# The load of the weight group two places on, tied behind the adding transfer of the next group

## The chip, the cores and the metric

The kernel runs on one core of a Trainium2 chip. The metric is the device time of one execution in microseconds: before the change the median of three runs is 1652.49 us (1649.63 to 1653.38). Engines are named as in the profile: PE (TensorE matmul), DVE (VectorE), ACT (ScalarE), POOL (GpSimd) and SP (SyncE). POOL, SP and ACT also issue DMA transfers.

## The reference

Two layers of a hybrid decoder over 512 tokens of width 2048, in float32. Each layer normalises its input, projects it with one wide matrix, runs three mixers side by side (a short gated convolution, a stick-breaking attention of 8 heads of 128, and a gated linear attention, GLA, of 4 heads), and projects their concatenation back into the residual stream.

```python
h = _rmsnorm(x, norm_g)
proj = h @ w_in
# proj is split into: cv_h cv_b cv_c cv_g | sb_q sb_k sb_v sb_g | gl_q gl_k gl_v gl_g gl_lr
y_conv = _short_conv(cv_h, cv_b, cv_c, conv_w, conv_b) * silu(cv_g)
q, k = _rmsnorm(sb_q, sb_qn_g), _rmsnorm(sb_k, sb_kn_g)
y_sb = _stick_breaking(q, k, sb_v) * silu(sb_g)
g = log_sigmoid(gl_lr @ gla_w_up + gla_b_up) / 16
y_gla = _rmsnorm(_gla(gl_q, gl_k, gl_v, g), gla_on_g) * silu(gl_g)
return x + concatenate([y_conv, y_sb, y_gla]) @ w_out
```

## The kernel before

The weights stream from HBM in groups of 256 columns (2048 x 256 float32, 2 MB, tile `st`, two buffers). `specs` lists them in the order of use: in each layer six groups of the GLA, then conv h 0, c 0, g 0, b 0, then for j = 0 to 3 the attention's v j, g j, q j and k j (two heads each), then conv h 1, c 1, g 1, b 1, and eight groups of `w_out`. I call the group by these names.

Each float32 operand is split into two float16 parts, and a product is three float16 matmuls. Two ways exist. A plain group (`project_cols`, `project_toks`; the values' groups v j and conv h 1 are such) multiplies directly. A group in `quick` (every g j, q j and k j of the attention, and some of the convolution) uses seven half-size products of sums of quarter blocks instead of eight (`project_quick`, lines 763 to 807: L778 and L781 are its matmuls).

What a weight group goes through, by lines:

- `fetch(i)` loads it in two halves of 1 MB (L360), issued on POOL's queue for all but the first three groups.
- `wmax(i, h)` squares it on ACT in two passes and sums (L379); for a quick group, between the two passes, POOL issues the **adding transfer** (L382): a DMA inside `st` that adds the left 128 columns of every second row block to the right 128 columns, in place. It is one of the sums that the seven products need, done by DMA.
- `wscale(i)` reduces the sums across partitions on POOL (L395, `wgm`) and makes a power-of-two scale on DVE (L398, L407, L411 `ws`, L413 `wu`).
- A plain group is then split by `whi` and `wlo` (L450 on ACT, L457 on DVE). A quick group is split by `wsums`: each of seven blocks goes through L500 on ACT (high part) and L501 on DVE (low part), with sums of blocks between them (L520, L522, L525 on DVE). L520 reads what the adding transfer wrote. The first two blocks don't need it.

When a group's matmuls begin, `weights()` takes it and does two things for the groups behind it: it issues the load of the group two places on (into the buffer that the group in use has left free, since its parts are split by then), and puts into `hooks` the squares and the scale and split of the next group, which are emitted behind the group's first matmul and behind a matmul in its middle.

In the attention, PE runs v j, then scores of heads of the pair before (L1249), g j, scores, q j, values (L1289), k j, values. Keys and queries of 512 tokens are normalised on DVE (L217 to L222, L1344 to L1357), split (L1361 on ACT, L1362 on DVE) and transposed by DMAs that SP issues (L1366: `qT<-qp` the queries, `kT<-raw` the keys). So in the values' group v j+1 the keys of pair j are being normalised and transposed, the weights of g j+1 are being scaled and split, and the scores of pair j follow right behind the group. `mixd` transfers (L900) are finished mixer outputs on their way to HBM, on POOL's queue too.

The order on each engine comes from a scheduler that orders instructions by a simulated timeline. What is emitted inside `tc.high_priority()` is preferred. `order(a, b)` makes the scheduler place a behind b; between two engines it adds no wait at run time, on one engine it fixes their order.

Of the kernel before, what the change touches and what calls it, by code (L numbers as in the profile page):

```python
# [11 lines left out]
ALU = mybir.AluOpType  # L12
# [5 lines left out]
P = 128  # L18
# [25 lines left out]
def hybrid_trunk(ctx, tc, x, norm_g, w_in, conv_w, conv_b, sb_qn_g, sb_kn_g,  # L44
                 gla_w_up, gla_b_up, gla_on_g, w_out, out):
    nc = tc.nc
    V, S, G, T = nc.vector, nc.scalar, nc.gpsimd, nc.tensor
# [4 lines left out]
    HK = KT // 2  # L52
    GW = 256
# [17 lines left out]
    def nm(s):  # L71
        uid[0] += 1
        return f"{s}_{uid[0]}"

    def sm(n, tag, bufs=None):
        return small.tile([P, n], F32, tag=tag, name=nm(tag), bufs=bufs or 1 + (tag in TWICE))

    def wk(shape, tag, bufs=None, dt=F32):
        return work.tile(shape, dt, tag=tag, name=nm(tag), bufs=bufs)
# [115 lines left out]
    def order(a, b):  # L195
        tc.add_manual_dep(a.ins, b.ins.name, mybir.DependencyInfo(
            mybir.DependencyClass.NoSync, mybir.DependencyReason.DATA), reason="order")
# [116 lines left out]

    quick = set()
    specs = []

    def spec(name, l, src, cols):
        if name in (QUICK[l] if src is w_out else QUICK_IN):
            quick.add(len(specs))  # L320
        specs.append((l, src, cols))

    for l in range(depth):
        for name, cols in (("gla v 0", [(GL_V, GW)]), ("gla v 1", [(GL_V + GW, GW), (GL_LR, LR)]),
# [19 lines left out]
    staged, whole, narrow, peak, scales = {}, {}, {}, {}, {}  # L344

    def junk(n):

        return wk([P, HK * GX], "junk", 1, dt=U8)[:, :n]


    def fetch(i):

        l, src, cols = specs[i]
        queue = nc.gpsimd if i > 2 else nc.sync
        staged[i] = st = []
        whole[i] = stage.tile([P, KT, GW], F32, tag="st", name=nm("st"))
        for h in range(2):
            s_ = whole[i][:, h * HK:(h + 1) * HK, :]
            c0 = cols[0][0]
            queue.dma_start(s_, src[l, h * HK * P:(h + 1) * HK * P, c0:c0 + GW].rearrange("(k p) n -> p k n", p=P),  # L360
                            max_dma_last_dim=1024)
            st.append(s_)
        if len(cols) > 1:
            c0, w = cols[1]
            narrow[i] = wk([P, KT, w], "kT")
            nc.sync.dma_start(narrow[i], src[l, :, c0:c0 + w].rearrange("(k p) n -> p k n", p=P))

    def early(i):
        return i in quick and specs[i][1] is not w_out

    def wmax(i, h):

        if h == 0:
            peak[i] = sm(2 + (i in narrow), "wm")
        if early(i):
            part = whole[i][:, :, (1 - h) * P:(2 - h) * P]
        else:
            part = staged[i][h]
        sq = S.activation(junk(HK * GW).rearrange("p (k n) -> p k n", k=part.shape[1]), part, AF.Square,  # L379
                          accum_out=peak[i][:, h:h + 1])  # L380
        if early(i) and not h:
            G.dma_start(out=whole[i][:, ::2, P:], in_=whole[i][:, ::2, :P], accum_op=ALU.add)  # L382
        if h and i in narrow:
            S.activation(junk(KT * LR).rearrange("p (k n) -> p k n", k=KT), narrow[i], AF.Square,
                         accum_out=peak[i][:, 2:3])
        return sq
# [55 lines left out]
        else:  # L442
            V.tensor_scalar(wh[:, ks, :GW], staged[0][h][:, ks, :GW], scales[0], None, ALU.mult)

    hooks, lastmm = [], [None]

    def whi(i, h):
        wh = wpool.tile([P, HK, GX], F16, tag="wh", name=nm("wh"))
        wl = wpool.tile([P, HK, GX], F16, tag="wl", name=nm("wl"))
        hi = S.activation(wh[:, :, :GW], staged[i][h], AF.Copy, scale=scales[i])  # L450
        if i in narrow:
            S.activation(wh[:, :, GW:], narrow[i][:, h * HK:(h + 1) * HK, :], AF.Copy, scale=scales[i])
        loaded[i][0].append((wh, wl))
# [8 lines left out]
    def squares(i, mm):  # L462

        with tc.high_priority():
            for h in range(2):
                a = wmax(i, h)
                if not h:
                    order(a, mm)

    def parts_of(i, mm):  # L470

        with tc.high_priority():
            order(wscale(i), mm)
            if i in quick:
                wsums(i)
                return
            for h in range(2):
                whi(i, h)
                wlo(i, h)
# [49 lines left out]
    def weights():  # L529

        i = cursor[0]
        cursor[0] += 1
        if i + 2 < len(specs):
            with tc.high_priority():
                fetch(i + 2)
        assert not hooks
        if i and i + 1 < len(specs):
            hooks.extend([lambda mm: squares(i + 1, mm), lambda mm: parts_of(i + 1, mm)])
        return loaded.pop(i)

    fetch(0)
# [128 lines left out]
    for l in range(depth):  # L670
# [207 lines left out]
        def mixscale(j, m, tag, top=11.0):  # L878

            pow2(pmix[:, j:j + 1], m, -top, tag)  # L880
            s_ = sm(1, tag + "smix")
            V.reciprocal(s_, pmix[:, j:j + 1])
            return s_
# [103 lines left out]
        for tag in ("qT", "kT"):  # L987
# [10 lines left out]
            s_ = sm(1, "gas")  # L998
# [41 lines left out]
        for p in range(2):  # L1040
# [53 lines left out]
            for two, bias in ((0, (nT[:, p, 0:1], None, nT[:, p, 2:3], None)),  # L1094
                              (1, (nT01[:, p:p + 1], nT[:, p, 1:2], None, nT[:, p, 2:3]))):
                e = wk([P, 2, 256], "e")
                n = [0, 0]
# [201 lines left out]
        for j in range(4):  # L1299
# [17 lines left out]
            s_ = mixscale(2 + j, m, "b", 12.0)  # L1317
# [140 lines left out]
```

## Time and profile before

| | |
|---|---|
| median of three runs | 1652.49 us (1649.63 to 1653.38) |
| the profiled execution's own time | 1652.11 us |
| its span, first to last instruction | 1650.3 us |
| granted PE clock, mean | 0.999 |
| bytes moved by DMA | 234.90 MB, mean 142 GB/s |
| of them by POOL's queue (q0) | 177.22 MB, 39.9% of 16 engines' span |
| loads of `w_in` on POOL's queue (L360) | 114 halves of 1 MB |
| adding transfers (L382) | 34 of 512 KB |

A profile's span is given as busy time of each engine and as the idle time ahead of each instruction with what ended it. A row of a timeline reads: start and length in us, engine, line, operation, what it writes and reads, shape, how often, and in brackets the idle time of the engine ahead of it and what ended it. A row that ends in "x2" merges two equal ones. A row of POOL or SP with DMA in its name is the time of the issue, not of the transfer. A row of the waits reads: who waited, for what, in total, how often, the longest.

### The profile page before, as it was taken

To read this page: it belongs to the slowest core of one execution; us is meant where nothing else is said; L and a number is where in the kernel's file an instruction comes from. 1 tells how busy PE (TensorE), PEld (TensorE's weight loads), DVE (VectorE), ACT (ScalarE), POOL (GpSimd) and SP (SyncE) were. 2 spreads that over 40 slices of the span, in tenths; PEclk is the share of its full clock that TensorE was granted. 3 is DMA by queue.
4 is the path that set the end of the run, shared out by engine and by line. 5 is a ranking of instruction groups with operands and counts; after the bars stand their busy time and mean duration, and the time that the engine had idled before them with its cause. 6 is when DMAs were issued, how large, how long until landed. Compare 5 with 4: busy or idle time off the path is not lost.

```text
span 1650.3 us, 41607 instructions
## 1 busy us (share of the span) xinstructions
PE 1621.0 (98%) x17914; PEld 1341.0 (81%) x17914; DVE 1415.1 (86%) x2377; ACT 1185.3 (72%) x1743; POOL 270.0 (16%) x298
## 2 busy tenths in 40 slices
PE   7999999999999999999999999999999999999999
PEld 5746668988999968789986467689898989668998
DVE  7977989969797979798689689898898989888893
ACT  8667787857777776756765687788786868666571
POOL 0121121111212121111112112112121212111110
PEclk9999999999999999999999999999999999999999
DMA  7144344496767686644543442635777766683441
GB/s 260 58 150 122 70 133 86 111 159 148 167 148 167 148 167 175 170 157 149 193 141 104 115 116 66 178 78 151 148 163 150 161 155 150 158 229 129 154 155 53
DMA packets 193913, 234.90 MB, mean 142 GB/s; under 512 B 90226, under 2 KB 154044, under 8 KB 193216
## 3 DMA queue, kind: packets, MB, share of 16 engines
q0 software_dynamic: 76992, 177.22, 39.9%
q1 hardware_dynamic: 107728, 45.56, 13.7%
q10 hardware_dynamic: 9008, 9.45, 1.8%
q8 instruction: 140, 2.29, 0.6%
q14 instruction: 45, 0.37, 0.1%
HBM read 179.65 MB, written 14.68 MB: 118 GB/s over the span
## 4 chain that ended last, share of the span: by engine, by line
PE 40%; DVE 5%; ACT 3%; DMA 1%; issue 1%; POOL 0%; DVEq 0%; ACTq 0%; POOLq 0%
PE psp L781 11%; PE psp L778 7%; PE psp L828 5%; PE psp L697 3%; PE psp L698 3%; PE psp L699 3%; PE psp L686 3%; PE psp L687 3%; PE psp L688 2%; DVE wl L501 1%; ACT junk L379 1%; ACT wh L500 1%; DVE za L1265 1%; PE psm L1289 1%; DMA st<-in_w_in_dram 1%
## 5 line engine op out<-in xcount | busy, mean ns | idle before, releaser
L500 ACT ACTIVATE wh<-st,ws 128x1024 f16<-128x1024 f32 x252 | 281.7, 1147 | 194.0 <-DVE st L520 96.7
L501 DVE SCALAR_TENSOR_TENSOR wl<-st,ws,wh 128x1024 f16<-128x1024 f32 x252 | 318.0, 1283 | 37.9 <-ACT wh L500 37.8
L379 ACT ACTIVATE junk<-st 128x2048 uint8<-128x2048 f32 x150 | 285.7, 1905 | 16.7 <-DMA st<-in_w_in_dram 8.5
L778 PE MATMUL psp<-s,wh 128*128 128x256 f16 x1152 | 195.6, 273 | 0.0
L778 PEld LDWEIGHTS <-wh 128*128 128x128 f16 x1728 | 168.3, 98 | 22.4 <-issue 2.1
L781 PE MATMUL psp<-wh,s 128*128 128x128 f16 x2048 | 176.7, 219 | 0.0
L697 PE MATMUL psp<-wh,m 128*128 128x256 f16 x640 | 174.5, 273 | 0.0
L698 PE MATMUL psp<-wl,m 128*128 128x256 f16 x640 | 174.5, 273 | 0.0
L699 PE MATMUL psp<-wh,m 128*128 128x256 f16 x640 | 174.5, 273 | 0.0
L781 PE MATMUL psp<-wl,s 128*128 128x128 f16 x1024 | 173.2, 219 | 0.0
L781 PEld LDWEIGHTS <-s 128*128 128x128 f16 x3072 | 172.9, 98 | 0.0
L457 DVE SCALAR_TENSOR_TENSOR wl<-st,ws,wh 128x2048 f16<-128x2048 f32 x68 | 158.9, 2347 | 14.7 <-ACT wh L450 14.7
L450 ACT ACTIVATE wh<-st,ws 128x2048 f16<-128x2048 f32 x66 | 130.7, 1998 | 41.8 <-DVE ws L411 22.8
L360 POOL DMA_DIRECT2D st<-in_w_in_dram x114 | 102.7, 905 | 344.3 <-DVE w7l L501 119.9
L778 PE MATMUL psp<-s,wl 128*128 128x256 f16 x576 | 156.7, 273 | 0.0
L395 POOL PARTITION_ALL_REDUCE wgm<-wm x75 | 54.3, 724 | 489.9 <-ACT junk L379 477.2
L781 PEld LDWEIGHTS <-m 128*128 128x128 f16 x2304 | 131.1, 98 | 2.2 <-issue 1.6
L382 POOL DMA_DIRECT2D st<-st x34 | 53.8, 1584 | 276.5 <-ACT junk L379 236.1
L778 PEld LDWEIGHTS <-wl 128*128 128x128 f16 x864 | 84.5, 98 | 16.0 <-issue 6.0
L781 PE MATMUL psp<-wh,m 128*128 128x128 f16 x1024 | 91.5, 219 | 0.3 <-DVE raw L794 0.3
L781 PE MATMUL psp<-wl,m 128*128 128x128 f16 x512 | 87.5, 219 | 0.0
L688 PEld LDWEIGHTS <-wl 128*128 128x128 f16 x448 | 43.8, 98 | 53.7 <-DVE wl L457 2.3
(442 smaller groups left out, 4203.0 us busy)
## 6 DMA issues: line engine op xcount, KB each, us to landing
st<-in_w_in_dram POOLq DMA_DIRECT2D x114, 1024.0 KB, 8.2
st<-in_w_out_dram POOLq DMA_DIRECT2D x32, 1024.0 KB, 8.4
st<-st POOLq DMA_DIRECT2D x34, 512.0 KB, 7.0
st<-in_w_in_dram SPq DMA_DIRECT2D x6, 1024.0 KB, 11.8
mixd<-g POOLq DMA_DIRECT2D x20, 256.0 KB, 6.9
x<-in_x_dram SPq DMA_DIRECT2D x4, 1024.0 KB, 5.1
qT<-in_x_dram ACTq DMA_DIRECT2D x8, 512.0 KB, 6.2
qT<-xs ACTq DMA_DIRECT2D x8, 512.0 KB, 3.9
```

Of the source, the lines that this page charges most:

```text
L360: queue.dma_start(s_, src[l, h * HK * P:(h + 1) * HK * P, c0:c0 + GW].rearrange("(k p) n -> p k n", p=P), max_dma_last_dim=1024)
L379: sq = S.activation(junk(HK * GW).rearrange("p (k n) -> p k n", k=part.shape[1]), part, AF.Square, accum_out=peak[i][:, h:h + 1])
L450: hi = S.activation(wh[:, :, :GW], staged[i][h], AF.Copy, scale=scales[i])
L457: V.scalar_tensor_tensor(wl[:, :, :GW], staged[i][h], scales[i], wh[:, :, :GW], ALU.mult, ALU.subtract)
L500: hi = S.activation(h_, b, AF.Copy, scale=sc)
L501: V.scalar_tensor_tensor(l_, b, sc, h_, ALU.mult, ALU.subtract)
L697: T.matmul(o, ah[:, t, k, :], wh[:, kk, :n], start=st_, stop=False, skip_group_check=True)
L698: T.matmul(o, ah[:, t, k, :], wl[:, kk, :n], start=False, stop=False, skip_group_check=True)
L699: return T.matmul(o, al[:, t, k, :], wh[:, kk, :n], start=False, stop=en, skip_group_check=True)
L778: mm = T.matmul(o, w[q_][:, kk, :], a[p_][:, :, kk, :], start=st_, stop=en, skip_group_check=True)
L781: mm = T.matmul(o[:, t * P:(t + 1) * P], a[p_][:, t, kk, :], w[q_][:, kk, :], start=st_, stop=en, skip_group_check=True)
L828: mm = T.matmul(o[:, :n], a_[:, t, k, :], w[k // HK][part][:, k % HK, :n], start=i == 0 and k == 0, stop=i == 2 and k == KT - 1)
```

## The change

In the groups whose name begins with "v " and in conv h 1 (`held`), the load of the group two places on is no longer emitted at the start of `weights()`. It is emitted behind the group's first matmul, right after the next group's squares, with `order` behind the last adding transfer that was emitted (`added[0]`), which is that of the next group: g j, or conv c 1. All other groups load as before.

```diff
     quick = set()
     specs = []
+    names = []
 
     def spec(name, l, src, cols):
         if name in (QUICK[l] if src is w_out else QUICK_IN):
             quick.add(len(specs))
         specs.append((l, src, cols))
+        names.append(str(name))
...
-    def fetch(i):
+    def fetch(i, behind=None):
...
-            queue.dma_start(s_, src[l, h * HK * P:(h + 1) * HK * P, c0:c0 + GW].rearrange("(k p) n -> p k n", p=P),
-                            max_dma_last_dim=1024)
+            load = queue.dma_start(s_, src[l, h * HK * P:(h + 1) * HK * P, c0:c0 + GW].rearrange(
+                "(k p) n -> p k n", p=P), max_dma_last_dim=1024)
+            if behind is not None:
+                order(load, behind)
             st.append(s_)
...
         if early(i) and not h:
-            G.dma_start(out=whole[i][:, ::2, P:], in_=whole[i][:, ::2, :P], accum_op=ALU.add)
+            added[0] = G.dma_start(out=whole[i][:, ::2, P:], in_=whole[i][:, ::2, :P], accum_op=ALU.add)
...
-    hooks, lastmm = [], [None]
+    hooks, lastmm, added = [], [None], [None]
...
         i = cursor[0]
         cursor[0] += 1
-        if i + 2 < len(specs):
+        held = names[i][:2] == "v " or names[i] == "conv h 1"
+        if i + 2 < len(specs) and not held:
             with tc.high_priority():
                 fetch(i + 2)
         assert not hooks
+
+        def first(mm):
+            squares(i + 1, mm)
+            if held:
+                with tc.high_priority():
+                    fetch(i + 2, added[0])
+
         if i and i + 1 < len(specs):
-            hooks.extend([lambda mm: squares(i + 1, mm), lambda mm: parts_of(i + 1, mm)])
+            hooks.extend([first, lambda mm: parts_of(i + 1, mm)])
         return loaded.pop(i)
```

The built programs show what moves. The order of PE and of SP is the same in both. Line numbers of the changed kernel are 2 to 12 higher (L362 is L360 of before, L386 is L382, L399 is L395, L504 and L505 are L500 and L501, L1365 to L1374 are L1353 to L1362).

POOL in the values' group v 1 of layer 0, before: `st_4191` is the weight of g 1, `st_4599` that of q 1.

```order
L360 DMA st_4191<-in_w_in_dram 128x8x256 x2
L900 DMA mixd_187<-g_1488 1024x1x128
L360 DMA st_4599<-in_w_in_dram 128x8x256 x2
L382 DMA st_4191<-st_4191 128x8x128
L395 ISA wgm_4659<-wm_4607 128x2
L382 DMA st_4599<-st_4599 128x8x128
```

The same place in the changed kernel, where `st_4610` is the weight of q 1:

```order
L362 DMA st_4191<-in_w_in_dram 128x8x256 x2
L912 DMA mixd_187<-g_1488 1024x1x128
L386 DMA st_4191<-st_4191 128x8x128
L362 DMA st_4610<-in_w_in_dram 128x8x256 x2
L399 ISA wgm_4659<-wm_4604 128x2
L386 DMA st_4610<-st_4610 128x8x128
```

The load of q 1 and the adding transfer of g 1 have changed places; the reduction of g 1's maxima still follows both. The same swap stands in each of the ten held groups.

DVE in the same group, before: the end of the keys' norm (`qr`, `qrt`), the first low part of g 1 (`wl_4668`), then the scaling of the keys (L1357) and their low part (L1362).

```order
L222 SCALAR_TENSOR_TENSOR qr_467_4575<-qrt_4577,qr_467_4575 128x16
L220 TENSOR_TENSOR qrt_4577<-qr_467_4575 128x16
L501 SCALAR_TENSOR_TENSOR wl_4668<-st_4191,ws_4663,wh_4667 128x1024
L221 SCALAR_TENSOR_TENSOR qrt_4577<-qrt_4577,qrm_3777 128x16
L222 SCALAR_TENSOR_TENSOR qr_467_4575<-qrt_4577,qr_467_4575 128x16
L1353 TENSOR_SCALAR qz_4587<-qr_467_4575,qu_4181 128x8
L1355 TENSOR_SCALAR qr_467_4575<-qr_467_4575,wu_3893 128x8
L1354 TENSOR_SCALAR qz_4587<-qz_4587 128x8
L1357 TENSOR_TENSOR kT_4190<-kT_4190,qr_467_4575 128x1024
L1362 SCALAR_TENSOR_TENSOR raw_4592<-kT_4190,raw_4592 128x1024
```

The same place in the changed kernel:

```order
L222 SCALAR_TENSOR_TENSOR qr_467_4575<-qrt_4577,qr_467_4575 128x16
L220 TENSOR_TENSOR qrt_4577<-qr_467_4575 128x16
L221 SCALAR_TENSOR_TENSOR qrt_4577<-qrt_4577,qrm_3777 128x16
L222 SCALAR_TENSOR_TENSOR qr_467_4575<-qrt_4577,qr_467_4575 128x16
L1365 TENSOR_SCALAR qz_4587<-qr_467_4575,qu_4181 128x8
L505 SCALAR_TENSOR_TENSOR wl_4668<-st_4191,ws_4663,wh_4667 128x1024
L1367 TENSOR_SCALAR qr_467_4575<-qr_467_4575,wu_3893 128x8
L1366 TENSOR_SCALAR qz_4587<-qz_4587 128x8
L1369 TENSOR_TENSOR kT_4190<-kT_4190,qr_467_4575 128x1024
L1374 SCALAR_TENSOR_TENSOR raw_4592<-kT_4190,raw_4592 128x1024
```

The low part of g 1 stands three rows later, still ahead of the scaling of the keys. The four rows of g 1's scale (L398 to L413) stand a few rows later as well, between the steps of the norm.

ACT in the values' group v 2 of layer 0, before, with `wh` the high parts of g 2 and `raw` the high part of the keys of pair 1:

```order
L897 ACTIVATE g_3538<-e_6015,bsmix_3774 128x512
L500 ACTIVATE wh_6107<-st_5607,ws_6103 128x1024
L1361 ACTIVATE raw_6008<-kT_5606 128x1024
L500 ACTIVATE wh_6109<-st_5607,ws_6103 128x1024
L500 ACTIVATE wh_6107<-st_5607,ws_6103 128x1024
```

The same place in the changed kernel:

```order
L909 ACTIVATE g_3538<-e_6015,bsmix_3774 128x512
L1373 ACTIVATE raw_6008<-kT_5606 128x1024
L504 ACTIVATE wh_6107<-st_5607,ws_6103 128x1024
L504 ACTIVATE wh_6109<-st_5607,ws_6103 128x1024
L504 ACTIVATE wh_6107<-st_5607,ws_6103 128x1024
```

The split of the keys has gone ahead of the first high part. DVE follows it at this place: there L1357 and L1362 stand ahead of the first L501. So it is in v 2, v 3 and conv h 1 of both layers; v 0 has no difference on ACT or DVE.

## The prediction

> **What bounds the kernel now.** I read the page's busy times first, then the windows view over the stretches that the change touches, then the waits of PE, and last the timelines.
>
> ```profile
> PE 1621.0 (98%) x17914; PEld 1341.0 (81%) x17914; DVE 1415.1 (86%) x2377; ACT 1185.3 (72%) x1743; POOL 270.0 (16%) x298
> ```
>
> PE is busy for 1621.0 of 1650.3 us. Whatever the change does to loads, DVE or ACT counts only where PE waits, and the change doesn't touch the order of PE's instructions. So the question is where PE is idle in the changed stretches. The windows view answers it. Each row below is one stretch from the start of a values' group to the start of the next, or of conv h 1 (first column its bounds, then its length, then busy time of each engine): the first three begin with v 1, v 2 and v 3 of layer 0, the last three with those of layer 1.
>
> ```profile
> core 0: us, PE busy (x) PEld busy (x) DVE busy (x) ACT busy (x) POOL busy (x), PEclk, DMA share, GB/s
> 336.10:426.20 90.10, 84.29 (x1095) 78.00 (x1093) 74.04 (x123) 63.45 (x112) 15.21 (x18) 1.00 0.78 148
> 426.20:509.80 83.60, 83.60 (x1096) 77.95 (x1093) 74.36 (x124) 63.71 (x109) 16.32 (x18) 1.00 0.71 152
> 509.80:593.40 83.60, 83.60 (x1095) 77.95 (x1093) 74.33 (x124) 64.03 (x109) 16.52 (x18) 1.00 0.71 157
> 1150.50:1234.50 84.00, 83.66 (x1096) 77.96 (x1094) 74.20 (x123) 63.52 (x112) 15.42 (x18) 1.00 0.76 158
> 1234.50:1318.10 83.60, 83.60 (x1096) 77.92 (x1093) 74.35 (x123) 63.94 (x109) 15.96 (x18) 1.00 0.73 153
> 1318.10:1401.70 83.60, 83.60 (x1096) 77.95 (x1094) 74.36 (x123) 63.92 (x109) 16.34 (x18) 1.00 0.69 158
> ```
>
> Four equal pieces of work take 83.60 us with PE busy throughout, the first one of layer 1 takes 84.00, and the first one of layer 0 takes 90.10. So **the most that any change of these loads can win is 6.50 + 0.40 = 6.9 us**, and nearly all of it lies in one stretch. The waits of PE from 320 to 440 us name what it is made of:
>
> ```profile
> PE psz L1249 <- DMA kT<-raw: 2.8, 2, 2.3
> PE psp L778 <- DVE g L794: 1.6, 1, 1.6
> PE psp L781 <- ACT wh L500: 0.8, 1, 0.8
> PE psp L781 <- DVE raw L794: 0.7, 1, 0.7
> ```
>
> 2.8 us go to the scores of pair 0, whose transposed keys land late; 1.6 + 0.8 + 0.7 = 3.1 us go to ACT and DVE that are behind. Why they are behind stands in the timeline of that stretch (start, length, engine, line, tiles, and in brackets the idle time ahead and what ended it) and in the DMA view of 330 to 362 us:
>
> ```profile
> 335.25 1.77 POOL L360 DMA_DIRECT2D st<-in_w_in_dram  x2 [3.91 <-DVE wl L457]
> 341.14 1.59 POOL L382 DMA_DIRECT2D st<-st  x1 [4.13 <-ACT junk L379]
> st<-in_w_in_dram POOLq DMA_DIRECT2D x2, 1024.0 KB, 16.5
> st<-st POOLq DMA_DIRECT2D x1, 512.0 KB, 17.6
> 358.82 1.23 DVE L520 TENSOR_TENSOR st<-st 128x1024 f32<-128x1024 f32 x1 [5.59 <-DMA st<-st]
> 360.08 1.15 ACT L500 ACTIVATE wh<-st,ws 128x1024 f16<-128x1024 f32 x1 [8.26 <-DVE st L520]
> 362.65 1.90 ACT L379 ACTIVATE junk<-st 128x2048 uint8<-128x2048 f32 x1
> ```
>
> The load of q 1 (2 MB) is issued at 335.25, the adding transfer of g 1 behind it at 341.14, and it lands 17.6 us later. DVE's L520 needs its sum and stands for 5.59 us, ACT behind DVE for 8.26. In the other stretches this wait does not occur; there PE hides everything.
>
> **The change, part by part.** It makes five loads in each layer (after v 0 to v 3 and conv h 1) go behind the adding transfer of the next group. On POOL that is a swap of two neighbours; DVE and ACT change only in four windows of each layer; PE and SP not at all. No instruction is added or removed.
>
> (1) *The adding transfer goes first.* Its own issue does not move: at 341.14 POOL waited for ACT's L379, not for the load. What moves is what lies in POOL's DMA queue ahead of it. The DMA view of the whole run gives the medians from issue to landing:
>
> ```profile
> st<-in_w_in_dram POOLq DMA_DIRECT2D x114, 1024.0 KB, 8.2
> st<-st POOLq DMA_DIRECT2D x34, 512.0 KB, 7.0
> qT<-qp SPq DMA_TRANSPOSE x16, 7.1
> kT<-raw SPq DMA_TRANSPOSE x16, 5.1
> ```
>
> At 7.0 us it lands at about 348.1. DVE's first pieces ahead of L520 end at about 353.2 (358.82 less its 5.59 of idle time), so the wait of 5.59 us goes. What is late next there is DVE's own work: L520 starts at about 353.4. How much PE gets of this, layer 1 shows, where the same instructions ran with the addition landed in time:
>
> ```profile
> 1164.61 2.63 SPq L1366 DMA_TRANSPOSE kT<-raw  x2
> 1167.08 1.23 DVE L520 TENSOR_TENSOR st<-st 128x1024 f32<-128x1024 f32 x1
> PE psp L781 <- DVE raw L794: 0.3, 1, 0.3
> 1171.43 0.38 PE L1249 MATMUL psz<-kT,qT 128*128 128x512 f16 x1
> ```
>
> Counted from the start of its values' group, L520 stands there at 1167.08 - 1150.50 = 16.6 us; in layer 0 after the change at 353.4 - 336.1 = 17.3. There only 0.3 us of the later waits is left (the third row). I take 0.4 for layer 0, so of the 3.1 us **2.7 go**.
>
> (2) *The load goes 5 to 7.5 us later* (from 335.25 to 342.7 in this stretch, when the adding transfer is issued). Its first reader is the squares' pass of q 1, ACT's L379 at 362.65 above; the load, 8.2 us a half and behind the addition, lands by about 354. In the later groups the room is less:
>
> ```profile
> 424.96 1.77 POOL L360 DMA_DIRECT2D st<-in_w_in_dram  x2 [2.66 <-DVE kT L801]
> 428.27 1.59 POOL L382 DMA_DIRECT2D st<-st  x1 [1.54 <-ACT junk L379]
> 443.44 1.90 ACT L379 ACTIVATE junk<-st 128x2048 uint8<-128x2048 f32 x1
> 447.37 2.19 ACT L500 ACTIVATE wh<-st,ws 128x1024 f16<-128x1024 f32 x2 [1.94 <-PE psp L699]
> ```
>
> In v 2's group the load would be issued at 429.9 and 430.8, and by the median with 3 us for the addition ahead of it (an estimate: half of a landing of 7.0) it lands by 430.8 + 8.2 + 3 = 442.0. The pass over it stands at 443.44, and ACT has 1.94 us of idle time behind it. Cost: nothing; if that cover is gone, ACT's lateness goes on at one us for one us into parts of q that PE reads only in its next group.
>
> (3) *The keys' transposes run beside the load* instead of beside the addition. That is what decides over the 2.8 us, and over the other groups:
>
> ```profile
> 333.25 9.73 SPq L1366 DMA_TRANSPOSE qT<-qp  x2
> 350.81 6.51 SPq L1366 DMA_TRANSPOSE kT<-raw  x2
> 359.49 0.38 PE L1249 MATMUL psz<-kT,qT 128*128 128x512 f16 x1 [2.26 <-DMA kT<-raw]
> 435.57 4.03 SPq L1366 DMA_TRANSPOSE kT<-raw  x2
> 447.17 0.38 PE L1249 MATMUL psz<-kT,qT 128*128 128x512 f16 x1
> ```
>
> In layer 0's first stretch PE could have begun at 359.49 - 2.26 = 357.2. The transposes were issued from 350.81 and took 6.51 us on SP alone, with the load and then the late addition beside them. After the change the addition is gone by then and the end of the load is beside them. In layer 1 the same pair was ready within 1171.43 - 1164.61 = 6.8 us; issued at 351.0 (0.2 later, since DVE's four rows of the weight scale stand a little later) that gives 357.8, 0.6 after PE is ready. The upper bound is a pair as slow as before, 2.8 us; the lower is no wait. I take 0.8, near layer 1's row: **2.0 of the 2.8 us go**. In the six other groups of this kind PE has room: both are issued by 435.57 + 4.03 = 439.6, the second lands at latest 5.1 later, 444.7, and PE asks at 447.17, so 2.5 us are left. Medians of transposes beside a load (qT, 7.1) and beside an addition (kT, 5.1) differ by 2.0, which is hidden. Only layer 1's first group has no such room: its pair is ready at 1171.0 by the same sum, 0.4 ahead of PE. Between 0 and 2.0 - 0.4 = 1.6 us I take **0.4 us of loss**, as the load there is mostly in by then.
>
> The Trainium skill, "DMA: Bandwidth & Descriptors", section "Queues, rings and completion order", says that each DMA engine goes round the queues that have work, one whole packet from each. By that rule the transposes on SP's queue share every engine with POOL's load for as long as it lasts, wherever it stands, and the loss of part (3) would come in each of the eight groups. The medians of 7.1 and 5.1 us agree in direction; whether the rule bites on PE is the second rival below.
>
> (4) *The weight scale of g and its first pieces.* In v 2, v 3 and conv h 1, DVE now does the normalisation of k ahead of the scale, and ACT splits k (L1361) ahead of the first piece of g (L500). The first pieces come some 2.7 us later, but the second waited for PE anyway:
>
> ```profile
> 432.83 1.15 ACT L500 ACTIVATE wh<-st,ws 128x1024 f16<-128x1024 f32 x1 [1.19 <-DVE ws L411]
> 434.49 1.06 ACT L1361 ACTIVATE raw<-kT 128x1024 f16<-128x1024 f32 x1 [0.50 <-DVE kT L1357]
> 436.89 1.15 ACT L500 ACTIVATE wh<-st,ws 128x1024 f16<-128x1024 f32 x1 [1.34 <-PE psp L699]
> ```
>
> With L1361 done at 434.49 + 1.06 = 435.55, the first piece runs to 436.7 and the second starts at 436.9 as now: from there the order is the old one. Nothing for PE, whose g group begins only after the scores at 447.17. POOL's reduction of the maxima stands behind the load's two issues, so it comes at most 1.77 us later; the same cover holds.
>
> **Sum.** Layer 0: -2.0 (keys) - 2.7 (backlog) = -4.7. Layer 1: +0.4. Together -4.3 us against the profiled execution's own 1652.11 us (span 1650.3 and 1.8 around it), which lies 0.4 under the median of the three runs shown: **1647.8 us**.
>
> **The rivals.** *First, the keys stay late.* In layer 0's first stretch the load now beside them holds the transposes as long as load and addition did, so the 2.8 us stay and only the backlog goes, with the 0.4 of layer 1 lost: 1652.1 - 2.7 + 0.4 = 1649.8. For it: qT's pair of 9.73 us ran beside a load. Against it: half of that load is in by 351.
>
> *Second, slower: the transposes late in every group.* They share the engines with the load, and where a pair gets longer by more than the 2.5 us of room, PE waits. At 3.5 us more it would be 1.0 in each of six groups, 3.5 - 0.4 = 3.1 in layer 1's first, none won on the keys of layer 0: 1652.1 + 6.0 + 3.1 - 2.7 = 1658.5. For it: 9.73 against 4.03 us on SP shows that a pair can be 5.7 longer. Against it: the medians say 2.0.
>
> *Third, it doesn't do what it says.* The addition was late not for what stood ahead of it but since the DMA engines stood still. The DMA view of 330 to 362 us, 40 slices of 0.8 us, has a hole from about 338 to 345:
>
> ```profile
> GB/s 138 384 384 328 369 333 271 405 310 134 47 99 36 20 75 64 22 37 88 90 326 301 309 194 298 370 328 261 172 153 139 16 148 172 177 239 258 51 0 0
> ```
>
> If this hole stays and wanders to the addition, the stretch stays at 90 us: 1652. Against it: it ends by 346, and the addition alone, 3 us of work, would still be in by 350, ahead of the 353.4 at which it is asked for.
>
> *Fourth, all of it goes*: 1652.1 - 6.9 = 1645.2, both first stretches at 83.60.
>
> **How the numbers follow.** Forecast 0.50 (1646 to 1649.2), keys late 0.27, without effect 0.10, slower 0.07, all of it 0.06. The range runs from 1645.2 to 1653.5, no change and 1.4 above it, as the three runs of before reach 0.9 above their median; it leaves out the slower rival and the fringes. A measurement of this kernel can tell about 0.2%, 3.3 us, from no change. Against the median of 1652.49 that puts the bound at 1649.2: faster 0.55 (the forecast but for its fringe, and the fourth), within it 0.38, slower 0.07.
>
> **What would show it.** Right: the stretch from v 1 to v 2 of layer 0 takes 84 to 86.5 us instead of 90.1, DVE's L520 has no wait for the adding transfer, which lands 7 to 9 us after its issue, and the other stretches stay at 83.6. Step (3) is wrong if PE's wait for kT at L1249 stays at 2 us or turns up in the later groups; step (2) if ACT's L379 waits for a load in v 2 or v 3; step (4) if PE waits for g's pieces (L500 or L501). The forecast falls if the addition still lands late, or if layer 1 loses more than 1.6 us.

## The result, and the profile after

The changed kernel takes **1647.32 us** (median of 20 runs, 1645.52 to 1653.36) against 1652.65 us (20 runs, 1647.82 to 1659.48) for the kernel before: ratio 0.9967, 95% interval 0.9955 to 0.9978. The forecast was 1647.8. The profiled execution took 1647.99 us, its span is 1646.2, 4.1 us under that of before. Two executions of the experiments below ran clearly slower than the others of their kernel (3177.16 us in E6, 1671.59 in E11); they count in the medians given, and not in the ratios.

The windows view of the changed kernel, over the same six stretches as in the prediction (length, then busy time of PE, PE's loads, DVE, ACT, POOL):

```profile
336.70:421.00 84.30, 83.72 (x1095) 77.89 (x1093) 74.06 (x123) 63.37 (x112) 14.80 (x16) 1.00 0.75 158
421.00:504.60 83.60, 83.60 (x1096) 77.98 (x1094) 74.72 (x124) 63.71 (x108) 15.99 (x17) 1.00 0.75 151
504.60:588.20 83.60, 83.60 (x1097) 77.95 (x1095) 74.62 (x124) 63.99 (x109) 16.36 (x17) 1.00 0.74 159
1144.10:1229.40 85.30, 83.92 (x1096) 77.97 (x1094) 74.05 (x123) 63.69 (x112) 15.79 (x16) 1.00 0.75 156
1229.40:1313.80 84.40, 83.76 (x1096) 77.93 (x1094) 74.69 (x123) 63.60 (x108) 16.17 (x17) 1.00 0.76 150
1313.80:1397.40 83.60, 83.60 (x1096) 77.98 (x1094) 74.51 (x123) 63.92 (x109) 16.37 (x17) 1.00 0.74 160
```

v 1 of layer 0 went from 90.1 to 84.3 us. In layer 1, v 1 went from 84.0 to 85.3 and v 2 from 83.6 to 84.4. The other three stay at 83.6. The timeline of the first stretch (start, length, engine, line; in brackets the idle time ahead and what ended it):

```profile
333.82 5.43 SPq L1378 DMA_TRANSPOSE qT<-qp  x2
341.51 1.58 POOL L386 DMA_DIRECT2D st<-st  x1 [9.61 <-ACT junk L383]
342.42 2.49 POOL L362 DMA_DIRECT2D st<-in_w_in_dram  x2
351.25 4.53 SPq L1378 DMA_TRANSPOSE kT<-raw  x2
353.71 1.22 DVE L524 TENSOR_TENSOR st<-st 128x1024 f32<-128x1024 f32 x1
354.97 1.15 ACT L504 ACTIVATE wh<-st,ws 128x1024 f16<-128x1024 f32 x1 [2.71 <-DVE st L524]
357.54 1.90 ACT L383 ACTIVATE junk<-st 128x2048 uint8<-128x2048 f32 x1
```

The adding transfer is issued at 341.51, ahead of the load. DVE's L524 (L520 of before), which stood for 5.59 us, does not wait, and ACT waits 2.71 us instead of 8.26. What is left of PE's waits in this stretch, and the only wait for keys that is left in the run (layer 1), from the waits of PE:

```profile
PE psp L793 <- DVE raw L806: 0.5, 1, 0.5
...
PE psz L1261 <- DMA kT<-raw: 1.4, 2, 1.0
```

And the DMA view, the stretch's two rows first (median from issue to landing), then the whole run's:

```profile
st<-in_w_in_dram POOLq DMA_DIRECT2D x3, 1024.0 KB, 10.3
st<-st POOLq DMA_DIRECT2D x2, 512.0 KB, 7.0
...
qT<-qp SPq DMA_TRANSPOSE x16, 6.7
kT<-raw SPq DMA_TRANSPOSE x16, 9.6
```

The addition of g 1 lands 7.5 us after its issue instead of 17.6 (the row's 7.0 is the median of it and of the next group's, which took 6.5). Over the whole run the keys' transposes land in 9.6 us instead of 5.1: the load is now beside them.

All this looks like the prediction's own story, a transfer that moved ahead in a queue. The experiments say otherwise.

### The profile page after: what moved, and what is told of

The parts are those of the page before. It is cut to its first block, busy times and chain, and to the rows that moved or that the text cites. A ratio compares the mean times of both kernels' runs of the same rounds, so it can differ in the third digit from the quotient of the medians.

```text
span 1646.2 us, 41605 instructions
## 1 busy us (share of the span) xinstructions
PE 1620.8 (98%) x17914; PEld 1341.2 (81%) x17914; DVE 1416.7 (86%) x2377; ACT 1184.1 (72%) x1743; POOL 264.8 (16%) x298
## 4 chain that ended last, share of the span: by engine, by line
PE 37%; DVE 7%; DMA 3%; ACT 2%; issue 1%; POOL 0%; DVEq 0%; ACTq 0%; POOLq 0%
PE psp L793 9%; PE psp L790 6%; PE psp L840 5%; PE psp L709 3%; PE psp L711 3%; PE psp L710 3%; PE psp L698 3%; PE psp L699 3%; PE psp L700 3%; DVE wl L505 2%; DMA st<-in_w_in_dram 1%; DMA th<-za 1%; DVE za L1277 1%; PE psm L1301 1%; DVE w7l L505 1%
## 5 line engine op out<-in xcount | busy, mean ns | idle before, releaser
L504 ACT ACTIVATE wh<-st,ws 128x1024 f16<-128x1024 f32 x252 | 281.2, 1145 | 174.4 <-DVE st L524 91.3
L505 DVE SCALAR_TENSOR_TENSOR wl<-st,ws,wh 128x1024 f16<-128x1024 f32 x252 | 317.3, 1280 | 31.1 <-ACT wh L504 31.0
L362 POOL DMA_DIRECT2D st<-in_w_in_dram x114 | 109.8, 1029 | 297.1 <-DVE w7l L505 111.9
L399 POOL PARTITION_ALL_REDUCE wgm<-wm x75 | 53.6, 715 | 477.0 <-ACT junk L383 463.8
L386 POOL DMA_DIRECT2D st<-st x34 | 54.0, 1589 | 310.5 <-ACT junk L383 270.1
L790 PEld LDWEIGHTS <-wl 128*128 128x128 f16 x864 | 84.6, 98 | 13.4 <-issue 3.5
L793 PE MATMUL psp<-wl,m 128*128 128x128 f16 x512 | 87.5, 219 | 0.0
```

The lines of the kernel that those rows point to most:

```text
L362: load = queue.dma_start(s_, src[l, h * HK * P:(h + 1) * HK * P, c0:c0 + GW].rearrange("(k p) n -> p k n", p=P), max_dma_last_dim=1024)
L504: hi = S.activation(h_, b, AF.Copy, scale=sc)
L505: V.scalar_tensor_tensor(l_, b, sc, h_, ALU.mult, ALU.subtract)
L790: mm = T.matmul(o, w[q_][:, kk, :], a[p_][:, :, kk, :], start=st_, stop=en, skip_group_check=True)
L793: mm = T.matmul(o[:, t * P:(t + 1) * P], a[p_][:, t, kk, :], w[q_][:, kk, :], start=st_, stop=en, skip_group_check=True)
```

## The experiments

Twelve kernels ran, in four sets. Times are medians of 12 executions (4 for E9). Each ratio is to the kernel before in the same set, with its 95% interval; it is not the plain quotient of the two medians.

**E1 and E2: one stretch alone, and all but it.** The condition `held` is the edit:

```diff
-        held = names[i][:2] == "v " or names[i] == "conv h 1"
+        held = names[i] == "v 1" and specs[i][0] == 0                                              # E1
+        held = (names[i][:2] == "v " or names[i] == "conv h 1") and (names[i], specs[i][0]) != ("v 1", 0)   # E2
```

> Only the load behind v 1 of layer 0 is held; the nine other loads are issued as before the change. Theory (the gain is the adding transfer of g 1 no longer behind the load in POOL's DMA queue, in this one stretch): v 1 to v 2 of layer 0 takes 84.4 us as in the changed kernel's profile (90.1 before), and layer 1 does not lose its 1.3 + 0.8 us, so the time is 0 to 2 us under the changed kernel, 1645 to 1647.5 us. Rival A (the gain comes from many small places, through contention of loads with transposes): less than half of the gain, 1650 us or more. Rival B (a random stall of the DMA engines in before, not the order): the stretch varies whatever the kernel.

> The nine other loads are held, the one behind v 1 of layer 0 is not. Theory: the stretch v 1 to v 2 of layer 0 stays near 90 us, DVE waits some 5 us for the adding transfer there, and layer 1 pays the 2.1 us that it pays in the changed kernel: 1652.5 to 1655 us. DVE and ACT stand there in a changed order (keys ahead of the first low part of g 1) without the swap on POOL, so if that order made the gain (rival), the stretch falls to 85 us here. Rival A (gain from many places): 1649 to 1651 us.

E1: 1647.67 us, ratio 0.9961 (0.9940 to 0.9981), the whole gain. E2: 1651.94, ratio 0.9978 (0.9959 to 0.9997). In E2 the stretch is as bad as before. The windows row of E2's v 1, and its addition in the DMA view:

```profile
338.80:428.70 89.90, 85.74 (x1097) 78.75 (x1095) 74.16 (x124) 64.15 (x112) 13.81 (x16) 0.98 0.79 150
...
st<-st POOLq DMA_DIRECT2D x1, 512.0 KB, 16.8
```

So the gain sits in the one stretch. Whether the order on DVE makes it, E2 cannot tell: against the expectation, DVE and ACT run this stretch in exactly the order of before: the two traces show the same sequence. E4 and E5 below settle it. E2's 0.2% is no more than an unchanged kernel shows in E11, so it is not shown to be a gain.

**E3: the load on another queue.** The kernel of before, with the load of q 1 (group 16 in order of use) issued at its old time into ACT's DMA queue, so that nothing of it is ahead of the addition in POOL's:

```diff
-        queue = nc.gpsimd if i > 2 else nc.sync
+        queue = nc.scalar if i == 16 else nc.gpsimd if i > 2 else nc.sync
```

> The kernel of before, but the load of q 1 (behind v 1 of layer 0) is issued by ACT into ACT's DMA queue at about its old time, so nothing of it lies ahead of the adding transfer in POOL's queue, while it is in flight beside it. Theory (order within one queue): the adding transfer lands in 7 to 11 us instead of 17.6, the wait of L520 is gone or under 1 us, and the stretch takes 84 to 87 us; time 1646.5 to 1650 us. Rival C (bytes, not order: the load must be out of the way, in whichever queue): the addition lands after 14 us or more, L520 waits 3 us or more, the stretch stays at 88 us or more, 1650.5 us or more.

1652.81 us, ratio 0.9996 (0.9974 to 1.0018): no gain. From its DMA view and DVE's timeline:

```profile
st<-st POOLq DMA_DIRECT2D x1, 512.0 KB, 15.3
...
358.19 1.22 DVE L520 TENSOR_TENSOR st<-st 128x1024 f32<-128x1024 f32 x1 [5.84 <-DMA st<-st]
```

With the load in another queue the addition still takes 15.3 us and DVE still stands for 5.84. **The place in POOL's queue is not needed for it**: the theory that I had put on record fell here. The stretch took 87.5 us. The hole is there as well: in the DMA view of 330 to 364 us the rate falls from 346 GB/s to 134, 48, 98, 94 and 186 between 339.4 and 343.6.

**E4: the kernel of before again.**

> The kernel of before, unchanged. Theory: the stretch v 1 to v 2 of layer 0 takes 88 to 91 us again, with the adding transfer landing 14 us or more after its issue. Rival B (a random stall of the DMA engines in the one profiled execution): the stretch takes 85 us or less, or the stall sits elsewhere. Time 1651 to 1654 us either way.

1653.70 us in the median, as expected. But its profiled execution was the fastest of its twelve (1647.71), and it was a surprise. Its windows row of v 1, POOL's and SP's timeline and DVE's:

```profile
337.50:421.90 84.40, 83.75 (x1096) 78.01 (x1094) 74.04 (x123) 63.46 (x112) 15.21 (x18) 1.00 0.74 157
...
334.62 5.52 SPq L1366 DMA_TRANSPOSE qT<-qp  x2
...
336.63 1.76 POOL L360 DMA_DIRECT2D st<-in_w_in_dram  x2 [3.92 <-DVE wl L457]
342.38 1.59 POOL L382 DMA_DIRECT2D st<-st  x1 [4.00 <-ACT junk L379]
...
354.50 1.22 DVE L520 TENSOR_TENSOR st<-st 128x1024 f32<-128x1024 f32 x1
```

The old order on POOL, DVE and ACT, the addition behind the load, and yet no wait at L520 and 84.4 us; the addition took 10.5 us. So the unchanged kernel, when this stretch goes well, is as fast as the changed one's profile (1647.99). What differs from the first profile is SP's row: 5.52 us for the issue of the two transposes of the queries, against 9.73. The single packets tell more. In the first profile of before, fifteen 4 KB packets of the load took over 2 us (up to 2.67) between 341 and 345, where the median load packet takes 0.19. In E4 none did. They fill the second half of the hole of 338 to 345 in the prediction's GB/s row. The new theory: **loads stall by chance while a transposing transfer is in flight**, and all that follows them is late.

**E5: the transposes moved, POOL left alone.** The kernel of before; the queries' transposes of pair 0 in layer 0 are issued behind a copy of one column of q 1's weights, which SP can issue only when the load has landed:

```diff
+                def turn(nT_=nT_, parts=parts):
+                    return [nc.sync.dma_start_transpose(nT_[:, i].rearrange("p t h c -> p (t h) c"), parts[:, i])
+                            for i in range(2)]
+                if l == j == n == 0:
+                    late.append(turn)
+                else:
+                    turn()
...
                 fetch(i + 2)
+                if i == 14:
+                    landed = nc.sync.dma_start(sm(1, "gb"), staged[16][1][:, HK - 1, GW - 1:])
+                    for t in late.pop()():
+                        order(t, landed)
```

> The kernel of before, with POOL's order untouched (load of q 1, then the adding transfer of g 1); instead the two transposes of the queries of pair 0 in layer 0 are put behind the landing of that load, by a copy of one column of it on SP's queue. So the load no longer runs beside a transposing transfer. Theory now (the load is stalled, in some executions, by transposes in flight beside it, and everything behind it is late): the load's packets stay under 1 us, the adding transfer lands 8 to 11 us after its issue although it is still behind the load, DVE's L520 does not wait, v 1 to v 2 of layer 0 takes 84 to 87 us; time 1647 to 1650.5 us, with no tail above 1655. Rival (the place in POOL's queue): the adding transfer lands after 14 us or more, L520 waits 3 us or more, 88 us or more, time 1651.5 us or more.

1647.45 us, ratio 0.9962 (0.9944 to 0.9980): the same gain as the change, with the addition behind the load as ever. Its windows row, SP's and POOL's timeline, the DMA view of the stretch and DVE:

```profile
336.70:421.10 84.40, 83.74 (x1095) 77.94 (x1093) 73.98 (x123) 63.39 (x112) 15.13 (x18) 1.00 0.69 158
...
346.38 0.53 SPq L537 DMA_DIRECT2D gb<-st  x1
347.10 2.72 SPq L1371 DMA_TRANSPOSE qT<-qp  x2
...
335.83 1.76 POOL L360 DMA_DIRECT2D st<-in_w_in_dram  x2 [3.92 <-DVE wl L457]
341.68 1.59 POOL L382 DMA_DIRECT2D st<-st  x1 [4.09 <-ACT junk L379]
...
st<-st POOLq DMA_DIRECT2D x2, 512.0 KB, 7.1
...
353.79 1.23 DVE L520 TENSOR_TENSOR st<-st 128x1024 f32<-128x1024 f32 x1
```

The load is issued at 335.83 as before, and is in by 346.38, when SP's copy of its last column is issued. The addition of g 1 lands in 7.4 us (the row's 7.1 is the median of it and of the next group's). Even the two transposes are issued in 2.72 us instead of 9.73. DVE and ACT run the stretch in the order of before, so their changed order isn't what makes the gain.

**E6, E7, E8: where to hold, on one chip.** E6 holds in layer 0 alone, E7 is the changed kernel again, E8 is E1 again.

```diff
+        held = (names[i][:2] == "v " or names[i] == "conv h 1") and not specs[i][0]      # E6
```

> The loads are held in layer 0 alone. If the 1.3 + 0.8 us that the profile of the changed kernel shows in layer 1 are a price of holding there, the two stretches of layer 1 from v 1 and v 2 fall back to 84.0 and 83.6 us and the time is 1 to 2 us under that of the changed kernel on the same chip; if they come with loads beside transposes of other places, whatever is held, the time is the same as the changed kernel's within 1 us.

> The changed kernel once more, on the chip of the others of this set. v 1 of layer 0 takes 84.4 us again with no packet of a load over 2 us there; layer 1's v 1 takes 85.3 us again, as its wait for the keys belongs to the held load; v 2 of layer 1 takes 83.6 if its 0.8 us came from a stall that strikes in some executions, 84.4 if it is a price of the change. Time 1646.5 to 1649 us.

> Only the load behind v 1 of layer 0 held, on the same chip as the changed kernel. If this stretch is all the gain and layer 1's held loads cost 1.3 us, it is 1 to 2 us faster than the changed kernel: 1645 to 1648 us. If holding elsewhere also keeps stalls away, it is 1 us or more slower than the changed kernel and its times spread more.

1648.84, 1647.62 and 1648.78 us; ratios 0.9969 (0.9951 to 0.9988), 0.9963 (0.9942 to 0.9985) and 0.9963 (0.9946 to 0.9980). They cannot be told apart, so the price that I expected in layer 1 does not show in the times. Layer 1's v 1 in E6, where nothing is held, and in E7, where it is:

```profile
1144.50:1230.00 85.50, 83.82 (x1095) 77.93 (x1093) 74.19 (x123) 63.64 (x112) 15.07 (x18) 1.00 0.79 156
...
1144.70:1230.40 85.70, 84.16 (x1097) 78.00 (x1095) 74.07 (x123) 63.77 (x112) 14.69 (x16) 1.00 0.79 156
```

Over the ten profiles in which that load is not held (before, E1, E3, E4, E5, E6, E8, E9, E11, E12) the stretch takes 84.0 to 90.4 us, 85.5 in the mean; in the three in which it is (the changed kernel, E2, E7), 85.1 to 85.7, 85.3 in the mean. The means hide two different things. PE waits for the keys there, 0.6 to 1.4 us in all, in each of the three profiles with the load held, and in three of the ten others (E3, E9 and E11; 0.3 to 2.6 us). The other waits among the ten are mostly for DVE and ACT, and E9's 90.4 is the longest; five of the ten stay at 84.6 or less, none of the three. So holding most likely costs some 1 us here for the keys and saves a larger loss now and then; three profiles don't settle the balance. The 0.8 us in v 2 of layer 1 did not come back in E7 (83.6): in the changed kernel's profile twelve load packets over 2 us stand there.

**E9 and E12: the same collision where there was none.** The kernel of before, with two transposes of the last low part on SP's queue in each of the eight quick groups of `w_out`, issued when the split is done, which is also when the load two groups on goes out. E12 copies the same bytes on the same queue without transposing.

```diff
             split(b22, 6)
+            for _ in range(2):
+                nc.sync.dma_start_transpose(wk([P, HK, P], "za", dt=F16),           # E9
+                                            parts[6][1].rearrange("p k c -> p (k c)"))
+                nc.sync.dma_start(wk([P, HK, P], "za", dt=F16).rearrange("p k c -> p (k c)"),   # E12
+                                  parts[6][1].rearrange("p k c -> p (k c)"))
```

> The kernel of before with transposes added where there were none: in the eight quick groups of w_out (four in each layer) two transposes of the last low part (128 x 1024 float16 each, into an unused tile, their result is not read) are issued on SP when the group's last split is done, which is also when the load two groups on is issued. Theory (a transposing transfer beside a load stalls the load's packets, by chance more or less): in these eight places packets of the loads take 1 us and more, in one or two of them over 2 us, none of which the kernel of before shows there; the landing of those loads gets 3 us or more longer; the time rises by 0 to 3 us, since those groups have room. Rival (the stall belongs to the attention's stretch, not to transposes): landings there stay at 8.5 us and packets at 0.2 us.

> As E9, but the sixteen added transfers copy the same 128 x 1024 float16 tile without transposing it: same places, same bytes, same queue. E9 took 1665.6 us and lost 6.3 us of PE time in w_out of layer 0 and 6.0 in layer 1, each behind a stall of one load beside such a pair. If transposing is what stalls loads, no load packet in w_out takes over 2 us here, landings of w_out's loads stay near 8.5 us (9.1 in E9, two of them over 14), and the time is that of before within 2 us: 1651 to 1655 us. If any transfer beside a load does it, two or more such stalls stand in w_out again and the time is 1660 us or more.

E9: 1665.62 us, ratio 1.0088 (1.0056 to 1.0120). E12: 1653.00, ratio 0.9989 (0.9973 to 1.0006). The same place in both: SP's timeline, the landing of the load beside it and of the added transfers, in E9 DVE's wait for them, and what PE waited for behind it, E9 first:

```profile
787.72 7.69 SPq L518 DMA_TRANSPOSE za<-w7l  x2
...
st<-in_w_out_dram POOLq DMA_DIRECT2D x2, 1024.0 KB, 15.5
za<-w7l SPq DMA_TRANSPOSE x2, 17.3
...
806.34 1.28 DVE L501 SCALAR_TENSOR_TENSOR w7l<-st,ws,w7h 128x1024 f16<-128x1024 f32 x1 [4.55 <-DMA za<-w7l]
...
PE psp L831 <- ACT wh L450: 4.6, 1, 4.6
```

```profile
785.51 1.12 SPq L518 DMA_DIRECT2D za<-w7l  x2
...
st<-in_w_out_dram POOLq DMA_DIRECT2D x2, 1024.0 KB, 11.3
za<-w7l SPq DMA_DIRECT2D x4, 256.0 KB, 7.7
...
PE psp L831 <- ACT wh L450: 1.0, 1, 1.0
```

In E9 five of the eight pairs had a load issued within 1 us of them (at 766, 788, 808, 1586 and 1607); two of the five loads (788 and 1607) have packets over 2 us, up to 2.69 and 2.87, and PE loses 6.3 us behind the first and 6.1 behind the second, matmul by matmul against before. In E12 five pairs lie as near to a load; no load packet in `w_out` takes over 2 us, and the longest beside a pair takes 1.87.

The loss in E9, more than I had expected (0 to 3 us), is not the price of a late load alone. `w7l` has one buffer, so DVE's next last low part waits until the added transposes have read the old one: 4.55 us at the first place, 5.34 at the second, where ACT also stands 3.37 us for the load itself. The edit brought this wait in, and it bites because the transposes are as late as the load (17.3 us from issue to landing at the first place). The copies of E12 read `w7l` too, land in time, and the time stays that of before. Two stalls in five against none in five is little by itself; the times of all executions (E9 1662.4 us and more, E12 1656.6 and less) carry it. So the bytes alone don't do it. Whether it is the transposing or its small packets is open: by the packets of SP's queue a transpose moves its 256 KB in 1024 packets of 256 bytes, a copy in 128 of 2 KB.

**E10: both layers' queries late.** E5 with `i in (14, 52)`, so for v 1 of both layers.

> POOL's order of before; the queries' transposes of pair 0 are put behind the landing of the load in both layers (E5 did it in layer 0 alone). If the collision in v 1 is what costs, layer 1's v 1 takes 83.6 to 84.0 us without a stall of the load, layer 0's 84.4, and the time is that of E5 or up to 1 us less: 1646 to 1648 us. If waiting for the landing makes the queries or keys late, PE waits at the scores of layer 1 (its room there is 1.7 us before) and the time is 1 to 2 us above E5's.

1646.31 us, ratio 0.9975 (0.9958 to 0.9992), the lowest median of the study. The windows view has both stretches, 84.6 and 83.8:

```profile
336.00:420.60 84.60, 83.78 (x1096) 77.97 (x1094) 74.01 (x124) 63.36 (x112) 15.17 (x18) 1.00 0.69 158
1144.40:1228.20 83.80, 83.58 (x1095) 77.90 (x1093) 74.17 (x123) 63.38 (x112) 15.35 (x18) 1.00 0.71 159
```

That it beats the changed kernel (1647.32 and 1647.62) is not shown: the lead is less than the sets differ by, and against the kernel before of its own set it gains less (0.9975 against 0.9967 and 0.9963).

**E11: the kernel of before a third time.**

> The kernel of before once more, for another look at how often the stall strikes: of the three executions with a profile that had the load beside the queries' transposes of pair 0 on POOL's queue, two were stalled (90 us) and one was not (84.4). Theory: either of these two again, 84 to 85 us when no packet of the load takes over 2 us beside those transposes, 88 to 91 us when some do; time of the median 1652 to 1654 us.

1657.69 us against 1652.39 for the very same kernel in its set, ratio 1.0023 (1.0001 to 1.0045). The two medians of one kernel lie 5.3 us apart, as much as the change gains, so a single set proves little. The gain rests on seven kernels, none of which has the load and the transposes together in v 1 of layer 0 (the changed kernel, E1, E5, E6, E7, E8, E10): their ratios are 0.9961 to 0.9975, and those of the unchanged kernel are 0.9996 (E4) and 1.0023. Its profile, SP's row and PE's wait, is stalled again:

```profile
333.43 9.63 SPq L1366 DMA_TRANSPOSE qT<-qp  x2
...
PE psz L1249 <- DMA kT<-raw: 3.4, 2, 3.0
```

All fourteen profiles together, with v 1 of layer 0 measured from its first matmul to that of v 2, and the load packets over 2 us counted in it:

| what is in flight beside the load of q 1 | kernels | v 1 of layer 0 (us) | packets over 2 us |
|---|---|---|---|
| the queries' transposes | before, E2, E4, E9, E11, E12 | 90.1, 89.8, 84.4, 91.2, 90.9, 88.2 | 15, 30, 0, 15, 15, 15 |
| the same, load in 1 KB packets on ACT's queue | E3 | 87.5 | 0 (up to 1.98 us, median 0.05) |
| none; the load is held | after, E1, E6, E7, E8 | 84.4, 84.6, 84.4, 84.5, 84.3 | 0 in all |
| none; the transposes wait | E5, E10 | 84.5, 84.6 | 0 in both |

## Why the prediction was right, point by point

**The sum was right, and its largest term too.** -4.3 us was predicted for the profiled execution, -4.1 came (1652.11 to 1647.99). In layer 0's v 1, -4.7 was predicted and -5.7 came; in layer 1, v 1 and v 2 lost 2.1 together where 0.4 was predicted; the rest of the run came out 0.5 shorter. That the totals meet so closely is luck in part, the more so as an unchanged kernel's execution can differ from the first profile by 4.4 us (E4, 1647.71).

**Step (1), the addition goes first: its facts held, its reason did not.** The issue did not move (341.1 and 341.5), it lands in 7.5 us (7.0 forecast), L520 waits no more and starts at 353.7 (353.4 predicted), and of the 3.1 us of backlog 0.5 are left (0.4 predicted). But the step read the 17.6 us of before as the price of "what lies in POOL's DMA queue ahead of it". E3 took the load out of that queue and the addition took 15.3 us. E5 and E4 left it ahead, and the addition was in time. What made it late was a load stalled beside the queries' transposes. Holding the load cures this because its issue at 342 is behind those of the transposes (333.8 and 336.7), not because the addition goes first. The forecast of this step was met by luck: the same edit that reorders the queue happens to part the load from the transposes.

**Step (2), the load later costs nothing: right, and closer than it looked.** ACT's pass over the held weights waits for nothing in v 1 and v 2 of layer 0. In v 1 the load is in at 356.5, 1.0 us ahead of its reader at 357.54; the prediction compared it with 362.65, where that reader stood before, and left out that the gain brings the reader forward too. In v 3 the pass does wait:

```profile
523.14 1.91 ACT L383 ACTIVATE junk<-st 128x2048 uint8<-128x2048 f32 x1 [1.03 <-DMA st<-in_w_in_dram]
```

By the prediction's own test that counts against the step. PE does not feel it (83.6 us).

**Step (3), the keys beside the load: the direction right, the size too small.** In layer 0's v 1, 0.8 us of wait was left by the forecast; the waits of PE list none there. Where the room is wide the transposes got longer by far more than the 2.0 that I took: from the second issue to the last packet 3.0 to 5.0 us before, 7.9 to 9.2 after, in the six later groups. Of the room before PE's scores, 4.4 to 7.1 us then, 0.9 to 2.4 is left now. It stayed hidden by less than 1 us in three of them: the prediction had the room too small (2.5 us) as well as the lengthening, and the two misses cancelled. In layer 1's v 1 PE waits 1.4 us for keys, where 0.4 was taken and 1.6 was the bound. All three profiles with that load held have such a wait (0.6 to 1.4 us), three of the ten without, so the step had this cost right in kind.

**Step (4), the order on DVE and ACT: right.** The changed order runs in v 2 and v 3 of layer 0, and PE is busy throughout there (83.60 us each, as before).

**The rivals.** Late keys in every group (1658.5) did not come, but with under 1 us to spare. The third, "the DMA engines stood still", was closer to the cause than my forecast: the hole was the cause. I took the hole as something that would stay, and dismissed the rival because the addition alone would be in by 350 even so. The hole comes with the load and the transposes being in flight together, so the change removes it. What the prediction could not see was that one profile shows one draw: of six profiled executions with the old placement five have the stall. The spread of the times before (1647.8 to 1659.5, against 1645.5 to 1653.4 after) fits that, but isn't all due to this place: E1's profiled execution took 1652.59 us with 84.6 us in this stretch.

What remains open: why the stall strikes in most executions at this place and only in some at others of its kind (last section), whether the transposing or its small packets bring it about, and whether the holds in layer 1 pay.

## What to carry to other kernels

When one stretch among equals is slow, look at the single packets of the transfers in flight there before blaming the order of a queue, and take a second profile of the same kernel: a stall that comes by chance looks like structure in one. Keep large loads and transposing transfers apart in time where something waits for either of them; moving the load behind the transposes or the transposes behind the load gave about the same gain, 0.2 to 0.4%. Removing a collision that strikes in most executions lowers the median, even if no term of the busy time changes. And an experiment that adds transfers adds waits for their buffers: read which wait ends last before calling its cost the price of what it was meant to test.

## What the runs showed of the hardware that I had not expected

In the fourteen traces, 346 load packets of 4 KB took over 2 us, ten times and more the median of 0.19. They belong to 28 loads. **Every one of them lies beside a transposing transfer** (from 1.5 us ahead of its issue to 8 us behind the issue's end), although 47 to 60% of the load packets lie outside such times; the longest of those took 1.87 us. The stall holds the other side as well: in v 1 of layer 0 the issue of the second transpose takes 4.2 to 7.0 us on SP in the five stalled profiles, and 2.3 to 2.9 in E4 and where that load is held.

When the two are issued counts as well. Of the 1021 loads on POOL's queue in the fourteen traces, 271 have a transposing issue within 1.2 us of one of their own two issues, and 27 of these (10%) have packets over 2 us; of the 750 others one has, and that one follows at once on a stalled one. In v 2 of before the nearest issues are 2.6 us apart (422.3 and 425.0), and no packet is slow. This was found in the traces and not tried by itself, nor does it say why v 1 of layer 0 is hit five times in six and most places seldom.

The same bytes on the same queue without transposing cost no time (E12 against E9, 1653.0 and 1665.6 us). The Trainium skill's rule quoted in the prediction ("DMA: Bandwidth & Descriptors", "Queues, rings and completion order") tells how an engine shares its turns between queues, packet by packet; these runs add that in a stall a single 4 KB packet can take up to 4.09 us (E1). In "Advanced Engine Details and Errata", section "X-Bar Transpose (TRN2)", the Trainium skill says that transposing DMAs are as fast as regular ones. Away from loads the traces come near that: the last added pair, with no load within 14 us, lands in 3.9 us in E9 and in 2.9 in E12 (medians). Beside a load they don't: 17.3 us against 7.7, in the rows above.

In four of the five stalled stretches PE's clock went down as well: the granted clock was 0.98 in E2's v 1 (row above), E11's and E12's and 0.96 in E9's, and the same matmuls took 85.5 to 87.0 us of busy time, against 83.7 to 83.8 in the changed kernel, E4 and E5. In the first profile of before it stayed at 1.00.
